# Layer 0's output projection in eight pairs of stripes with seven half-size products each, with weight sums built in DRAM during layer 0

## The chip, the cores and the metric

The kernel runs on one core of one Trainium2 chip. The metric is the device time of one execution, in microseconds (us). Before the change it is 1852.44 us, the median of three runs (1849.99 to 1852.57). The core has five engines with a queue of instructions each, and every queue runs in the order in which the program was laid out: TensorE (PE in the profile, its weight loads PEld), VectorE (DVE), ScalarE (ACT), GpSimd (POOL) and SyncE (SP). SP, ACT and POOL also issue DMAs; 16 DMA engines move the data.

## The reference, cut to what matters

Two residual layers over T = 528 tokens (16 meta tokens and 512), width D = 2048. Layer 0 is the even one; its output projection is the matrix product that the change touches.

```
def even_mixer(hn, w_in, ...):
    glu_v, glu_g, gate_a, q, c, gate_b, qi, ki, wi = split_last(hn @ w_in, EVEN_SPLITS)
    ...
    a_out = silu(layer_norm(u, ln_g, ln_b)) * silu(gate_a)        # 8 blocks of 128 features
    ...
    b_out = b_out * silu(gate_b)                                  # 8 heads of 128 features
    return concatenate([a_out, b_out], axis=-1) @ w_out           # (528 x 2048) @ (2048 x 2048)

for layer in range(DEPTH):                                        # DEPTH = 2
    hn = rms_norm(h, norm_gain[layer])
    y = even_mixer(hn, ...) if layer % 2 == 0 else odd_mixer(hn, ...)
    h = h + y
return rms_norm(h, final_norm_gain)[:, N_META:]
```

## The kernel before, in words

Activations lie transposed: 128 features on the partitions, tokens along a row. A matrix product goes by *stripes* of 128 output features. `stripe` (called with a stripe number, such as S_GA for the gates of group A or S_OE for layer 0's output projection) loads 128x2048 weights in one DMA on SP (`load_raw`, L184), takes their square sum on ACT (L192), adds it over the partitions on POOL (L144), makes a power-of-two scale from it with small DVE instructions (L148, L199, L201), and splits each half of the weights into two f16 tiles: `wh` on ACT (L208) and `wl`, the rest, on DVE (L209). The activations are split in the same way into a high and a low f16 tile (L298 on ACT, L299 on DVE). Each of the 16 k-blocks of 128 then takes three matmuls (L251, L252, L253: high by high, high by low, low by high) in each of two column halves of 264 tokens, so a stripe has 96 matmuls of 264 columns. They write PSUM tiles named `mps`, of which there are three; `s1` (four) and `po` (one) are the PSUM tiles of the attention.

Layer 0 is written as a list of steps (`EVEN`): `g` is one GLU block with its convolution of 31 DVE instructions (L584), `s` one stripe of indexer queries with its scores, `k` the top-k choice, `h` one attention head with its gate (L594, L595, tile `gb`, two buffers), `n` the layer norm of group A. Behind the list come eight gate stripes of group A (S_GA, `gate`), each with five instructions that finish `MA[i]` (L707 to L711). Then all 16 inputs of the output projection are split (`MX`, L298 and L299): eight from attention, of which six were stored to DRAM (`mbd`) by their heads and are read back on SP at L739, and eight from `MA`. Then 16 stripes of the output projection run; each adds its result onto the residual `h1` on DVE (L780), squares the new residual on ACT (L786) and sums the squares on DVE (L787). Layer 1's first two weight stripes (L271, plain f32 matmuls, 128 of them) fill the time until the row norms are there (L309, L316, L317), and L298/L299 split the inputs of layer 1.

Layer 1's own output projection already goes by pairs: `pair_stripes` takes two stripes at a time with seven products of eight k-blocks and half of the tokens each (`product`, L1154, 24 matmuls each), where two stripes in the plain way are eight such products. Four of its seven weight operands are sums of weight blocks which DMAs on POOL have built in DRAM beforehand (`os` tiles, `sum_steps`, `waves`, `send`, L347; the add happens in the DMA).

A scheduler lays the program out. Each instruction has a priority by its `band` (weights 5, evacuations 4, side work such as attention 3, convolutions and sums 2), each engine's queue is then fixed, and a queue waits at its first instruction whose input is not there. `behind(...)` places an instruction after a named earlier one.

## Time and profile before

| | |
|---|---|
| median of three runs | 1852.44 us |
| the profiled execution | 1855.38 us, its span 1853.6 us |
| PE busy | 1818.7 us (98% of the span), granted clock 0.992 on average |
| DVE busy | 1337.6 us (72%) |
| ACT busy | 1191.4 us (64%) |
| POOL busy | 183.5 us (10%) |

The profiled execution is 2.9 us above the median. Stages of layer 0 in that execution, by the windows and the chain of waits: scores, GLU and convolutions to about 350 us, heads to about 690 us with the gate stripes among the last of them, the output projection from 716.4 to 889.1 us, and the layer boundary to about 930 us. "x" before a number is a count of instructions; PEclk is the granted TensorE clock as a share of full speed. Each digit of the page's slices is the busy share of one fortieth of the span in tenths:

```profile
PE   9999999999999989999999999999999999999997
PEld 6767577788888878888777777777777765446886
DVE  7699998997646565445587777777777776757775
ACT  4845565355555876443487877778777777865562
```

### The profile page before, as it was taken

To read this page: it belongs to the slowest core of one execution; us is meant where nothing else is said; L and a number is where in the kernel's file an instruction comes from. 1 tells how busy PE (TensorE), PEld (TensorE's weight loads), DVE (VectorE), ACT (ScalarE), POOL (GpSimd) and SP (SyncE) were. 2 spreads that over 40 slices of the span, in tenths; PEclk is the share of its full clock that TensorE was granted. 3 is DMA by queue.
4 is the path that set the end of the run, shared out by engine and by line. 5 is a ranking of instruction groups with operands and counts; after the bars stand their busy time and mean duration, and the time that the engine had idled before them with its cause. 6 is when DMAs were issued, how large, how long until landed. Compare 5 with 4: busy or idle time off the path is not lost.

```text
span 1853.6 us, 36583 instructions
## 1 busy us (share of the span) xinstructions
PE 1818.7 (98%) x14870; PEld 1412.4 (76%) x14870; DVE 1337.6 (72%) x2763; ACT 1191.4 (64%) x1937; POOL 183.5 (10%) x344
## 2 busy tenths in 40 slices
PE   9999999999999989999999999999999999999997
PEld 6767577788888878888777777777777765446886
DVE  7699998997646565445587777777777776757775
ACT  4845565355555876443487877778777777865562
POOL 1100100021212012000011011010100000001000
PEclk9999999999999989999999999999999999999998
DMA  5533223234344345334465455554555344556553
GB/s 201 160 99 101 93 76 121 97 112 124 107 129 111 103 126 187 126 118 156 116 216 168 141 174 156 183 164 144 171 149 171 115 159 166 195 187 238 200 188 112
DMA packets 64856, 271.68 MB, mean 147 GB/s; under 512 B 8208, under 2 KB 15672, under 8 KB 47568
## 3 DMA queue, kind: packets, MB, share of 16 engines
q1 hardware_dynamic: 35552, 179.28, 27.6%
q0 software_dynamic: 17616, 52.19, 11.9%
q10 hardware_dynamic: 11520, 37.88, 6.1%
q8 instruction: 116, 1.90, 0.4%
q14 instruction: 52, 0.43, 0.1%
HBM read 250.76 MB, written 40.04 MB: 157 GB/s over the span
## 4 chain that ended last, share of the span: by engine, by line
PE 90%; DVE 5%; ACT 2%; DMA 1%; issue 1%; SPq 0%; POOL 0%; ACTq 0%; DVEq 0%
PE mps L251 22%; PE mps L252 22%; PE mps L253 22%; PE mps L1154 8%; PE mps L271 2%; PE po L638 1%; PE s L271 1%; PE s L613 1%; DVE mask L559 1%; DVE m L558 1%; PE s L854 1%; PE s L853 1%; DVE wl L209 1%; PE s L855 1%; PE po L976 1%; PE po L975 1%
## 5 line engine op out<-in xcount | busy, mean ns | idle before, releaser
L251 PE MATMUL mps<-x,wh 128*128 128x264 f16 (+1 forms) x3168 | 942.2, 297 | 3.2 <-ACT gt L571 1.9
L252 PE MATMUL mps<-x,wh 128*128 128x264 f16 (+1 forms) x3168 | 942.0, 297 | 0.5 <-DVE x L299 0.5
L253 PE MATMUL mps<-x,wl 128*128 128x264 f16 (+1 forms) x3168 | 941.8, 297 | 0.0
L252 PEld LDWEIGHTS <-wh 128*128 128x128 f16 x3392 | 332.7, 98 | 119.0 <-issue 6.4
L253 PEld LDWEIGHTS <-wl 128*128 128x128 f16 x3392 | 332.6, 98 | 115.4 <-issue 2.6
L251 PEld LDWEIGHTS <-wh 128*128 128x128 f16 x3392 | 332.9, 98 | 113.0 <-issue 4.0
L208 ACT ACTIVATE wh<-w,sc 128x1024 f16<-128x1024 f32 x220 | 251.1, 1144 | 198.9 <-PE mps L252 175.8
L209 DVE SCALAR_TENSOR_TENSOR wl<-w,sc,wh 128x1024 f16<-128x1024 f32 x220 | 281.1, 1280 | 104.6 <-ACT wh L208 104.4
L192 ACT ACTIVATE junk<-w 128x2048 bf16<-128x2048 f32 (+1 forms) x114 | 210.9, 1850 | 12.2 <-DMA w<-in_w_dram 8.5
L584 DVE SCALAR_TENSOR_TENSOR z<-u,vec,z 128x528 f32<-128x528 f32 x240 | 181.1, 762 | 2.3
L144 POOL PARTITION_ALL_REDUCE tot<-ss x94 | 43.3, 461 | 843.7 <-ACT junk L192 843.6
L1154 PEld LDWEIGHTS <-wh 128*128 128x128 f16 x912 | 89.2, 98 | 11.0 <-issue 0.3
L208 ACT ACTIVATE wh<-w,oq 128x1024 f16<-128x1024 f32 x53 | 60.6, 1148 | 54.6 <-PE mps L1154 46.3
L209 DVE SCALAR_TENSOR_TENSOR wl<-w,oq,wh 128x1024 f16<-128x1024 f32 x53 | 67.8, 1282 | 28.1 <-ACT wh L208 28.0
L1154 PE MATMUL mps<-on,wh 128*128 128x256 f16 x464 | 78.2, 273 | 0.1
L192 ACT ACTIVATE junk<-gw 128x1024 bf16<-128x1024 f32 x64 | 66.9, 1045 | 2.0 <-DMA gw<-in_w_dram 1.6
L850 DVE SCALAR_TENSOR_TENSOR qlm<-q,qhm 128x256 f16<-128x256 f32 x128 | 52.4, 420 | 21.3 <-ACT qhm L849 21.3
L1154 PE MATMUL mps<-on,wl 128*128 128x256 f16 x232 | 63.2, 273 | 0.0
L849 ACT ACTIVATE qhm<-q 128x256 f16<-128x256 f32 x128 | 51.0, 411 | 17.5 <-DVE q L951 16.1
L251 PE MATMUL mps<-mx,wh 128*128 128x264 f16 x224 | 61.8, 276 | 0.0
L252 PE MATMUL mps<-mx,wh 128*128 128x264 f16 x224 | 61.8, 276 | 0.0
L253 PE MATMUL mps<-mx,wl 128*128 128x264 f16 x224 | 61.8, 276 | 0.0
(438 smaller groups left out, 2898.0 us busy)
## 6 DMA issues: line engine op xcount, KB each, us to landing
w<-in_w_dram SPq DMA_DIRECT2D x132, 1024.0 KB, 4.9
gw<-in_w_dram ACTq DMA_DIRECT2D x64, 512.0 KB, 6.3
os<-in_w_dram POOLq DMA_DIRECT2D x42, 512.0 KB, 8.2
w<-os SPq DMA_DIRECT2D x28, 512.0 KB, 4.5
w<-in_w_dram SPq DMA_DIRECT2D x23, 512.0 KB, 4.6
os<-os POOLq DMA_DIRECT2D x14, 512.0 KB, 5.9
h<-in_x_dram POOLq DMA_DIRECT2D x16, 264.0 KB, 5.5
h1d<-h ACTq DMA_DIRECT2D x16, 264.0 KB, 2.3
```

Source lines behind the costliest of these rows:

```text
L144: queued["G"] = G.partition_all_reduce(out, src, channels=128, reduce_op=op or bass_isa.ReduceOp.add)
L192: S.activation(junk[:, :src.shape[-1]], src, AF.Square, accum_out=ss)
L208: queued["S"] = S.activation(hi, src, AF.Identity, scale=sc)
L209: V.scalar_tensor_tensor(lo, src, sc, hi, op0=OP.mult, op1=OP.subtract)
L251: P.matmul(o, hi[half][:, ws], xh[:, sl], start=n == 0 and k == 0, stop=False)
L252: P.matmul(o, hi[half][:, ws], xl[:, sl], start=False, stop=False)
L253: P.matmul(o, lo[half][:, ws], xh[:, sl], start=False, stop=n == 1 and k == 7)
L271: queued["P"] = P.matmul(o[:m], w32[:, k * 128:k * 128 + m], X[k][:, sl], start=k == 0, stop=k == KT - 1)
L584: eng.scalar_tensor_tensor(z, u[:, j:j + T], col(V_CW + i * CW + j), z, op0=OP.mult, op1=OP.add)
L849: S.activation(hi, src, AF.Copy, scale=scale)
L850: V.scalar_tensor_tensor(lo, src, scale, hi, op0=OP.mult, op1=OP.subtract)
L1154: P.matmul(p, wt[:, sl], xt, start=start and k == i == 0, stop=stop and k == 7 and i == 2, skip_group_check=stop and not start and resume)
```

## The change

Layer 0's output projection is made of eight pairs of stripes with seven products each. With X11, X21 the first (group A or attention) halves of the inputs and the token halves t1 and t2, the code prepares four families of f16 inputs ("forms") instead of the 16 splits: PA (attention, t1 and t1 minus t2), PB, PC (mixtures over both halves) and PD (one half), each for eight blocks. They are made block by block as the gate stripes come: `attention_form(i)` and `mixed_forms(i)` in the loop over S_GA. The attention inputs come back from `mbd` by DMAs on POOL (L783) instead of SP. The tiles of the forms are memory that earlier stages have left (`slot`, `form`).

Four weight sums per pair are built in DRAM (`esum`), by 64 DMAs on POOL (L349, 512 KB each) which `send` issues during the steps of layer 0: one or two behind each GLU, head and early score stripe, the last four among the gate stripes. The square sums of the eight gate stripes' weights and of the first two pairs' are taken ahead: 24 loads of 512 KB on the ACT queue and 24 squares of 128x1024 on ACT (`foresee`, `foreseen`), so the gate stripes get scales that are known (`known=`) and have no square and no all-reduce of their own. The scale of the mixed inputs has a factor 16 more headroom.

A pair loads and splits seven half stripes (`half_load`, `split_weights`), takes 7 x 24 matmuls of 264 columns (`product`, L910 in the new code) and adds the products onto two residuals on DVE (`add`). For pairs 2 to 7 the four loads that give the scale are squared one pair ahead (`pair_begin`, called from `pair_rest`). The residual tiles and their row-square sums are as before.

```diff
+    esum = [[dram.tile([128, 1024], F32, name=f"es{p}{i}") for i in range(4)] for p in range(8)]
...
     def glu(i):
...
+        aside(i > 3)
         ps, inv = stripe(S_GLU + 2 * i + 1, X0, back0)
+        aside(i > 3)
...
-    def gate(s, dst, keep):
-        ps, inv = stripe(s, X0, back0, keep=keep)
+    def gate(s, dst, keep=None, known=None):
+        ps, inv = stripe(s, X0, back0, keep=keep, known=known)
...
+    def foresee():
+        with band(CONV), behind("S"):
+            while seen:
+                square_sum(*seen.pop(0))
+            if left:
+                s, n = left.pop(0)
+                raw = wide()[:, :1024]
+                S.dma_start(raw, w[s, :, 1024 * n:1024 * (n + 1)])
+                seen.append((raw, gas[:, 23 - len(left):24 - len(left)]))
...
+    def aside(late):
+        send(later, min(2 if late else 1, len(later) - 4))
+        if late:
+            foresee()
...
+    later = waves(S_OE, esum, 1024)
...
+    def stage(i):
...
+        with band(SIDE), behind("B6" if i < 4 else "B7"):
+            G.dma_start(XA[i], mbd[i])
...
+    def attention_form(i):
+        x = XA[i]
+        with band(SIDE):
+            V.tensor_tensor(x[:, t2], x[:, t1], x[:, t2], op=OP.subtract)
...
+            PA[i] = split(pairs_of[-1][:, i % 2], x, mxq[1])
+
+    def mixed_forms(i):
+        x, z = XA[i], MA[i]
+        with band(SIDE):
+            PB[i] = split(form(), z, mxq[0])
+            V.scalar_tensor_tensor(z[:, t2], x[:, t2], 2.0, z[:, t2], op0=OP.mult, op1=OP.add)
+            V.scalar_tensor_tensor(x[:, t1], x[:, t1], 2.0, z[:, t2], op0=OP.mult, op1=OP.subtract)
+            V.tensor_tensor(z[:, t1], z[:, t1], z[:, t2], op=OP.subtract)
+            PC[i] = split(form(), z, mxq[0])
...
+            PD[i] = split(form(True), x[:, t1], mxq[0])
...
     for i in range(8):
         ga = et([128, T], F32, "gb", 2)
-        gate(S_GA + i, ga, stat[:, 0, i:i + 1])
+        gate(S_GA + i, ga, known=(gasc[:, i:i + 1], gainv[:, i:i + 1]))
+        send(later, 1)
+        for n in ((0, 1, 2, 3), (4,), (5,), (), (), (), (6,), (7,))[i]:
+            stage(n)
+        if i < 6:
+            attention_form(i)
...
-            if i < 6:
-                Q.dma_start(mb, mbd[i])
-            MX[8 + i] = split(r1p.tile([128, 2, T], F16, name="mx" if i < 7 else "x", bufs=7 if i < 7 else KT), mb, c[7])
-        for i in range(8):
-            MX[i] = split(r1p.tile([128, 2, T], F16, name="x", bufs=KT), MA[i], c[6])
+        if i >= 6:
+            attention_form(i)
+        mixed_forms(i)
...
-    for n in range(KT):
...
-        ps, inv = stripe(S_OE + n, MX, mback, order=(1, 0))
...
+    def pair_begin(p):
+        w11, w12, w22 = w[S_OE + 2 * p, :, 1024:], w[S_OE + 2 * p, :, :1024], w[S_OE + 2 * p + 1, :, :1024]
+        with band(WGT):
+            w11, s1 = half_load(w11), half_load(esum[p][0])
...
+                with behind("S"):
+                    for i, v in enumerate((w11, s1, w12, w22)):
+                        square_sum(v, ss[:, i:i + 1])
...
+                all_sum(one[:, 1:2], one[:, 0:1])
+                sc, inv = scales(one[:, 1:2], mback)
...
+    def pair_corner(p, raw, scale, ring):
...
+        product(a, w11, x11)
...
+        product(c, s1, y1)
...
+    def pair_rest(p, raw, scale, banks, following):
...
+            s2, w12, s3 = [split_weights(v, sc) for v in vs[:3]]
+        nxt = pair_begin(following) if following < 8 else None
+        with band(WGT):
+            s4, w22 = [split_weights(v, sc) for v in vs[3:]]
+        for bank_, wt, xs, first, dst, scl in ((b, s2, u2, True, ha[:, t2], ninv), (a, w12, x21, False, ha[:, t1], inv),
+                                               (b, s3, z3, False, hb[:, t2], inv), (c, s4, x22, False, ha[:, t2], inv),
+                                               (b, w22, z4, False, hb[:, t1], inv)):
+            product(bank_, wt, xs, start=first)
+            with band(EVAC):
+                add(dst, bank_, scl)
```

**TensorE between the attention of heads 6 and 7.** Before, these rows stand together: `po_6937` and the `s1` tiles up to 7044 belong to head 6, those from 7298 on to head 7, and `mps_7925` is the second bank of a gate stripe.

```order
L635 MATMUL s1_7021<-ident_72,L_7001 128x128
L613 MATMUL s1_7034<-Kh_6608,qh_6934 16x16
L638 MATMUL po_6937<-pt_7014,Vt_6642 128x128 [waits Activation_49]
L638 MATMUL po_6937<-pt_7014,Vt_6642 128x128 x4
L644 MATMUL s1_7040<-ident_72,L_7031 16x16 [waits Activation_49]
L648 MATMUL s1_7044<-pt_7042,Vt_6642 128x16 [waits DVE_49]
L613 MATMUL s1_7298<-Kh_6625,qh_7290 128x144 [waits PE_49]
L631 MATMUL s1_7305<-ident_72,L_7294 128x128 [waits Activation_49]
L635 MATMUL s1_7308<-ident_72,L_7294 128x128
L613 MATMUL s1_7317<-Kh_6625,qh_7290 128x272 [waits DVE_49]
L638 MATMUL po_7293<-pt_7304,Vt_6643 128x128 [waits Activation_49,Pool_49]
```

In the changed program the same places of the two heads (line numbers 8 higher) read as follows, where `mps_8041` and `mps_8175` are banks of gate stripes:

```order
L253 MATMUL mps_8041<-x_374,wl_8049 128x264
L646 MATMUL po_7119<-pt_7196,Vt_6812 128x128 [waits Activation_49]
L646 MATMUL po_7119<-pt_7196,Vt_6812 128x128 x4
L652 MATMUL s1_7222<-ident_72,L_7213 16x16 [waits Activation_49]
L251 LDWEIGHTS wh_8048
L251 MATMUL mps_8041<-x_379,wh_8048 128x264
```

```order
L253 MATMUL mps_8175<-x_339,wl_8180 128x264
L656 MATMUL s1_7226<-pt_7224,Vt_6812 128x16 [waits DVE_49]
L621 MATMUL s1_7488<-Kh_6795,qh_7480 128x144 [waits PE_49]
L251 LDWEIGHTS wh_8179
L251 MATMUL mps_8175<-x_339,wh_8179 128x264
```

Between the first piece's `s1_7222` and the second's `s1_7226` stand 27 matmuls of gate stripes, and 39 more before head 7's first transposes; before the change none stood between any of the rows shown.

**VectorE at the end of the gate stripes.** Before, the last blocks are split one behind the other (`x` tiles from `z`), with one weight split among them:

```order
L299 SCALAR_TENSOR_TENSOR x_8510<-z_4510,mxb_8443,x_8510 128x528 [waits Activation_49]
L299 SCALAR_TENSOR_TENSOR x_8513<-z_4789,mxb_8443,x_8513 128x528 [waits Activation_49]
L209 SCALAR_TENSOR_TENSOR wl_8689<-w32_8671,sc_8680,wh_8688 128x1024 [waits PE_49,Activation_49]
L299 SCALAR_TENSOR_TENSOR x_8516<-z_5425,mxb_8443,x_8516 128x528 [waits Activation_49]
L710 SCALAR_TENSOR_TENSOR z_6511<-gt_8439,z_6511 128x528 [waits Activation_49]
L595 SCALAR_TENSOR_TENSOR gb_8313<-gb_8313,gt_8432 128x528 [waits Activation_49]
L711 TENSOR_TENSOR z_6511<-z_6511,gb_8313 128x528 [waits DVE_49]
L299 SCALAR_TENSOR_TENSOR x_8519<-z_6511,mxb_8443,x_8519 128x528 [waits PE_49,Activation_49]
```

In the changed program the last two blocks' forms stand among the weight splits of the first pairs (`mb` is the attention input of heads 6 and 7; L818 to L820 are the three mixing instructions):

```order
L852 TENSOR_TENSOR z_6681<-z_6681,gb_8579 128x528 [waits DVE_49]
L299 SCALAR_TENSOR_TENSOR x_8576<-mb_7211,mxb_7599,x_8576 128x264 [waits Activation_49]
L299 SCALAR_TENSOR_TENSOR Kh_8573<-z_5554,mxb_7599,Kh_8573 128x528 [waits Activation_49]
L209 SCALAR_TENSOR_TENSOR wl_8898<-w32_8884,gaq_616,wh_8897 128x1024 [waits DMAHW6_49,PE_49,Activation_49]
L299 SCALAR_TENSOR_TENSOR Vt_8702<-z_6681,mxb_7599,Vt_8702 128x528 [waits Activation_49]
L209 SCALAR_TENSOR_TENSOR wl_8929<-w32_8884,gaq_616,wh_8928 128x1024 [waits DMAHW7_49,PE_49,Activation_49]
L818 SCALAR_TENSOR_TENSOR z_6681<-mb_7575,z_6681 128x264 [waits DVE_49]
L819 SCALAR_TENSOR_TENSOR mb_7575<-mb_7575,z_6681 128x264 [waits DVE_49]
L820 TENSOR_TENSOR z_6681<-z_6681 128x264
L209 SCALAR_TENSOR_TENSOR wl_8933<-w32_8887,gaq_616,wh_8932 128x1024 [waits DMAHW1_49,PE_49,Activation_49]
L299 SCALAR_TENSOR_TENSOR x_8576<-mb_7575,mxb_7599,x_8576 128x264 [waits Activation_49]
L299 SCALAR_TENSOR_TENSOR x_8708<-z_6681,mxb_7599,x_8708 128x528 [waits Activation_49]
```

Before, the last low half of an input followed right behind the last gate's result (L711, now L852); now seven forms and mixes and three weight splits stand between the two.

**GpSimd in the middle of the heads.** Before, biases of the attention (`L<-bdram`, then the mask added) and the all-reduces of the weights' square sums follow each other:

```order
L605 DMA L_3722<-bdram_152 128x1x272 [waits DMASW5_49,PE_49,Activation_49]
L607 DMA L_3722<-mask1_577 128x272 [waits DMASW5_49]
L605 DMA L_3743<-bdram_152 128x1x400 [waits DMASW7_49,PE_49]
L144 ISA tot_5185<-ss_5182 128x1 [waits Activation_49]
L607 DMA L_3743<-mask2_580 128x400 [waits DMASW7_49,DMASW0_49]
L502 MEMSET Vt_3858 128x128 [waits PE_49]
L144 ISA tot_5307<-ss_5304 128x1 [waits Activation_49]
```

In the changed program steps of the sums (`es`) stand among them, some of which wait for the step before them:

```order
L613 DMA L_3791<-bdram_152 128x1x272 [waits DMASW5_49,PE_49,Activation_49]
L615 DMA L_3791<-mask1_577 128x272 [waits DMASW6_49,DMASW5_49]
L613 DMA L_3812<-bdram_152 128x1x400 [waits DMASW7_49,PE_49]
L615 DMA L_3812<-mask2_609 128x400 [waits DMASW7_49,DMASW0_49]
L507 MEMSET Vt_3927 128x128 [waits PE_49]
L144 ISA tot_5302<-ss_5299 128x1 [waits Activation_49]
L349 DMA es23_194<-in_w_dram 128x1024 [waits DMASW1_49]
L349 DMA es33_198<-es31_196 16x8192 [waits DMASW2_49]
L613 DMA L_3835<-bdram_152 128x1x528 [waits DMASW3_49,PE_49,Activation_49]
L615 DMA L_3835<-mask3_612 128x528 [waits DMASW4_49,DMASW3_49]
```

Two steps of the sums now stand between an all-reduce and the bias of this head's last block of queries, and each of the two waits for an earlier DMA of this queue.

More of the change, by code (lines that the diff above doesn't have):

```diff
@@ new lines, in trunk_kernel, with form, slot, get @@
+    whole, parts = [], []
+    def form(half=False):
+        if half:
+            return parts.pop(0)
+        if not whole:
+            return xp.tile([128, 2, T], F16, name="x", bufs=KT)
+        return whole.pop(0)()
+    def slot(name, shape, bufs, dt=F32):
+        def get():
+            t = et(shape, dt, name, bufs)
+            if len(shape) > 2:
+                t = t.rearrange("p a b -> p (a b)")
+            return t[:, :T].bitcast(F16).rearrange("p (a b) -> p a b", a=2)
+        return get
@@ L700, in trunk_kernel @@
+    pairs_of = []
+    whole.extend(slot(n, [128, T], 2, F32R) for n in ("ch", "ch", "cl", "cl"))
+    KV = [slot("Kh", [128, T], 3), slot("Vt", [128, 5, 128], 3)]
+    whole.extend(KV * 2)
+    whole.extend([slot("L", [128, T], 3)] * 3 + [slot("pt", [128, 5, 128], 2)] * 2 + KV)
+    for name in ("uh", "ul"):
+        u = E.tile([128, 1024], F32R, name=name, bufs=1).bitcast(F16)
+        parts.extend(u[:, c * T:(c + 1) * T].rearrange("p (a b) -> p a b", a=2) for c in range(3))
     MA = []
@@ new lines, in trunk_kernel, with half_load, product @@
+    spare = []
+    def half_load(src):
+        if not spare:
+            t = wpool.tile([128, 2048], F32, name="w32", bufs=3)
+            spare.extend((t[:, 1024:], t[:, :1024]))
+        t = spare.pop()
+        Q.dma_start(t, src)
+        return t
+    def product(p, ws, xs, start=True, stop=True, resume=True):
+        hi, lo = ws
+        for k in range(8):
+            sl = slice(k * 128, k * 128 + 128)
+            xh, xl = xs[k]
+            for i, (wt, xt) in enumerate(((hi, xh), (hi, xl), (lo, xh))):
+                P.matmul(p, wt[:, sl], xt, start=start and k == i == 0, stop=stop and k == 7 and i == 2,
+                         skip_group_check=stop and not start and resume)
@@ new lines, in cut, with add, first_square @@
+    def cut(X, sl):
+        return [(xh[:, sl], xl[:, sl]) for xh, xl in X]
+    def add(dst, p, scale):
+        V.scalar_tensor_tensor(dst, p, scale, dst, op0=OP.mult, op1=OP.add)
+    def first_square(n):
+        nonlocal done
+        if n == 0:
+            done = S.activation(acc1, HIN[n], AF.Square)
+        else:
+            sq = U.tile([128, T], F32, name="sq1", bufs=2)
+            done = S.activation(sq, HIN[n], AF.Square)
+            V.tensor_tensor(acc1, acc1, sq, op=OP.add)
+        S.dma_start(h1d[n], HIN[n])
@@ new lines, in pair_corner @@
+    def pair_corner(p, raw, scale, ring):
+        sc, inv, ninv = scale
+        with band(WGT):
+            w11, s1 = split_weights(raw[0], sc), split_weights(raw[1], sc)
+        with band(EVAC), behind("G"):
+            while len(HIN) < min(KT, 2 * p + 4):
+                residual0()
+        ha, hb = HIN[2 * p], HIN[2 * p + 1]
+        a, b, c = [ring()[:, :HT] for _ in range(3)]
+        product(a, w11, x11)
+        with band(EVAC):
+            c1 = U.tile([128, T], F32, name="sq1", bufs=2)[:, :HT]
+            S.activation(c1, a, AF.Identity, scale=inv)
+            V.tensor_tensor(ha[:, t2], ha[:, t2], c1, op=OP.add)
+            hb2 = hb.rearrange("p (a b) -> p a b", a=2)
+            V.tensor_tensor(hb2, hb2, c1[:, None, :].to_broadcast([128, 2, HT]), op=OP.subtract)
+        product(c, s1, y1)
+        with band(EVAC):
+            add(hb[:, t2], c, ninv)
+        return a, b, c
@@ new lines, in pair_rest @@
+    def pair_rest(p, raw, scale, banks, following):
+        sc, inv, ninv = scale
+        a, b, c = banks
+        d = esum[p]
+        ha, hb = HIN[2 * p], HIN[2 * p + 1]
+        with band(WGT):
+            vs = [half_load(v) if p < 2 or i in (0, 2, 3) else v
+                  for i, v in enumerate((d[1], raw[2], d[2], d[3], raw[3]))]
+            s2, w12, s3 = [split_weights(v, sc) for v in vs[:3]]
+        nxt = pair_begin(following) if following < 8 else None
+        with band(WGT):
+            s4, w22 = [split_weights(v, sc) for v in vs[3:]]
[3 more added lines that the diff above has]
+            product(bank_, wt, xs, start=first)
+            with band(EVAC):
+                add(dst, bank_, scl)
+                if wt is s4:
+                    first_square(2 * p)
+                elif wt is w22:
+                    first_square(2 * p + 1)
+        return nxt
@@ new lines, in trunk_kernel @@
+    mback = mxq[2]
+    done = None
+    H1 = HIN
+    x11, y1 = cut(PA, t1), cut(PA, t2)
+    x21, x22 = cut(PB, t1), cut(PB, t2)
+    z4, u2 = cut(PC, t1), cut(PC, t2)
+    z3 = PD
+    begun = [pair_begin(0), pair_begin(1)]
+    banks = [pair_corner(p, *begun[p], (bank, ps1)[p]) for p in range(2)]
+    for p in range(8):
+        if p > 1:
+            banks.append(pair_corner(p, *begun[p], bank))
+        nxt = pair_rest(p, *begun[p], banks[p], p + 2 if p == 0 else p + 1 if p > 1 else 8)
+        if nxt:
+            begun.append(nxt)
```

177 lines of the change are left out of this document (100 added, 77 removed).

## The prediction, as put on record

> **What bounds the kernel now.** I read the page's totals first, then the chain that ended last, then the windows of layer 0's end.
>
> ```profile
> span 1853.6 us, 36583 instructions
> PE 1818.7 (98%) x14870; PEld 1412.4 (76%) x14870; DVE 1337.6 (72%) x2763; ACT 1191.4 (64%) x1937; POOL 183.5 (10%) x344
> PE 90%; DVE 5%; ACT 2%; DMA 1%; issue 1%; SPq 0%; POOL 0%; ACTq 0%; DVEq 0%
> ```
>
> TensorE is busy for 98% of the span and makes 90% of the chain, so a matmul that goes away is worth its time wherever TensorE is the limit. Whether it is, has to be read stage by stage: columns are the stretch, its length, busy us and (instructions) of each engine, the granted clock, the DMA share and GB/s.
>
> ```profile
> 90.00:275.00 185.00, 181.93 (x1235) 127.12 (x1232) 178.18 (x316) 106.98 (x177) 21.01 (x33) 0.98 0.29 92
> 350.00:690.00 340.00, 331.25 (x2773) 285.91 (x2774) 235.52 (x494) 208.96 (x400) 59.56 (x95) 0.98 0.40 114
> 630.90:716.40 85.50, 80.83 (x658) 69.32 (x657) 48.03 (x108) 63.83 (x123) 18.94 (x34) 0.94 0.47 145
> 716.40:889.10 172.70, 172.70 (x1538) 150.20 (x1536) 79.95 (x137) 76.31 (x83) 7.94 (x19) 1.00 0.39 133
> 889.10:930.00 40.90, 40.33 (x184) 29.81 (x182) 25.89 (x44) 20.60 (x29) 4.51 (x8) 1.00 0.41 125
> ```
>
> The output projection is the row from 716.4 to 889.1: TensorE busy in all of it, at full clock, VectorE and ScalarE under half. The row ahead of it, head 7 and the gate stripes, has 4.7 us without matmuls and a clock of 0.94. From 90 to 275 us VectorE is nearly as full as TensorE (178.18 of 185).
>
> **The products: −21.6 us.** 16 stripes of 96 matmuls are 1536, in 172.70 us with two others: 0.1123 us each. Eight pairs of seven products of 24 matmuls, also 264 columns wide, are 1344. 192 fewer, at 0.1123 us, are 21.6 us. This holds if nothing else limits the new stage. The nearest stage that runs so is layer 1's output projection, with pairs and seven products of 256 columns:
>
> ```profile
> 1690.00:1830.00 140.00, 139.86 (x1279) 125.02 (x1278) 101.14 (x129) 80.03 (x91) 2.12 (x4) 1.00 0.53 183
> L208 ACT ACTIVATE wh<-w,sc 128x1024 f16<-128x1024 f32 x220 | 251.1, 1144 | 198.9 <-PE mps L252 175.8
> L209 DVE SCALAR_TENSOR_TENSOR wl<-w,sc,wh 128x1024 f16<-128x1024 f32 x220 | 281.1, 1280 | 104.6 <-ACT wh L208 104.4
> L192 ACT ACTIVATE junk<-gw 128x1024 bf16<-128x1024 f32 x64 | 66.9, 1045 | 2.0 <-DMA gw<-in_w_dram 1.6
> L780 DVE SCALAR_TENSOR_TENSOR h<-mps,inv,h 128x264 f32<-128x264 f32 x31 | 15.3, 492 | 29.2 <-PE mps L253 29.2
> L787 DVE TENSOR_TENSOR acc<-acc,sq 128x528 f32<-128x528 f32 x14 | 9.8, 702 | 1.4 <-ACT sq L786 1.4
> L786 ACT ACTIVATE sq<-h 128x528 f32<-128x528 f32 x14 | 8.8, 629 | 9.1 <-DVE h L780 9.1
> ```
>
> It shows no stall (139.86 of 140.00). Layer 0's pair has more beside it. TensorE takes 168 × 0.1123 = 18.9 us for a pair. VectorE: seven splits at 1.280 are 9.0 us, six additions at 0.492 are 3.0, two sums of squares at 0.702 are 1.4, the two instructions that spread the first product about 1.2 (one like L780, one like L787), and the small ones of the scale below 1: 15 to 15.6 us. ScalarE: seven splits at 1.144 are 8.0, four squares at 1.045 (5.0 with their readouts, at most 0.2 each), two row squares at 0.629 are 1.3, one evacuation 0.5: some 14.8 us. Both fit under 18.9, with a fifth to spare. I take no stall; what happens if that cover is gone is a rival below.
>
> **The hole between heads 6 and 7: −7 us.** Before, TensorE loses time in the gate stripes:
>
> ```profile
> 658.00:662.00 4.00, 2.61 (x21) 1.96 (x19) 1.13 (x6) 2.00 (x5) 1.46 (x2) 1.00 0.06 18
> 662.00:666.00 4.00, 2.73 (x13) 2.40 (x13) 1.06 (x5) 1.07 (x5) 1.23 (x3) 0.59 0.47 121
> 666.00:670.00 4.00, 1.99 (x7) 1.56 (x8) 2.88 (x8) 2.98 (x8) 1.38 (x2) 0.50 0.67 154
> 670.00:674.00 4.00, 4.00 (x23) 3.07 (x22) 3.54 (x9) 3.93 (x10) 0.84 (x2) 0.63 0.53 121
> ACT gb L594 <- DVE mb L649: 3.3, 1, 3.3
> PE s L631 <- ACT L L622: 9.0, 5, 2.8
> ```
>
> Busy time by granted clock is 2.61 + 2.73 × 0.59 + 1.99 × 0.50 + 4.00 × 0.63 = 7.7 us of full-speed work in 16 us, so 8.3 us are lost. The last two rows (time, times, longest) say why: a gate tile `gb` waits until head 6 has given one back, the gate stripe's second bank waits for it, and meanwhile TensorE's queue holds only the short dependent matmuls of the attention, each waiting for ScalarE's softmax. In the changed order 27 gate matmuls stand between two of these steps and 39 behind them, 66 × 0.1123 = 7.4 us of work. So the holes have something in them. I take 7; the bounds are 0, if those matmuls find their banks or weights not ready, and 8.3.
>
> Beside these rows stands a rule of the Trainium skill, page "TensorE: Matmul & The Clock Gate", Part 1 (the HAM clock gate): after about 3.4 us of an idle window the clock goes to half, and about 3.4 us of work bring it back. The rows with 0.59 and 0.50 agree with it, and by it a filled hole returns all of the slow matmuls, so that this term would be −8.3 and the sum 1.3 us lower; a new wait of that length would cost 1.7 us more than itself (half of 3.4, an estimate).
>
> **The forms: +5 us.** Rows for their prices, two of them from layer 1's forms of 256 columns, and the reload of an attention block (KB, us to landing):
>
> ```profile
> L298 ACT ACTIVATE x<-z,mxb 128x528 f16<-128x528 f32 x7 | 4.6, 719 | 0.0
> L299 DVE SCALAR_TENSOR_TENSOR x<-z,mxb,x 128x528 f16<-128x528 f32 x7 | 4.9, 761 | 1.2 <-ACT x L298 1.2
> L1061 DVE TENSOR_TENSOR on<-on 128x256 f32<-128x256 f32 x3 | 1.3, 425 | 0.1
> L1063 DVE TENSOR_TENSOR on<-on,on 128x256 f32<-128x256 f32 x3 | 1.3, 418 | 0.0
> Kh<-mbd SPq DMA_DIRECT2D x3, 264.0 KB, 2.6
> ```
>
> For each block VectorE does three wide low halves (3 × 0.761 = 2.3 us), one narrow one and four narrow mixes (five instructions; 0.42 from layer 1's rows to 0.49 from L780, so 2.1 to 2.5). Eight blocks are 35 to 38 us; the 16 old low halves at 0.761 were 12.2. So 23 to 26 us are added. ScalarE gets three wide and one narrow, 2.6 × 8 = 21 us, for 16 × 0.719 = 11.5, and loses the eight full squares of the gate stripes. On the whole stage from 630.9 to 716.4, VectorE's 48.03 us become 71 to 74 in the 78.5 us that are left without the hole: it fits, at over 90%. But the mixes cannot be spread: the changed order puts 111 VectorE instructions from the end of head 6's attention to the last form, worth 60 to 66 us at this trace's durations for each kind, against some 61 us of matmuls up to the product that needs that form. Two waits more stand on this path. VectorE's subtraction on a reloaded attention block is queued behind a DMA that GpSimd issues only after head 7's last bias, and all of VectorE's queue waits with it (the same reload took 2.6 us to land from SP's queue; I allow 2 to 3.5); and the last low half comes after three weight splits (3 × 1.280). Bounds: 0, when the order's excess is absorbed by the two corners of products that run first on attention forms alone (96 matmuls, 10.8 us), and 12, when the excess of 6, the wait of 3.5 and one more round of 2.5 add up. I take 5, nearest the order's own sum.
>
> **The sums in DRAM and the early squares: +3 us.** Prices per transfer:
>
> ```profile
> q1 hardware_dynamic: 35552, 179.28, 27.6%
> q0 software_dynamic: 17616, 52.19, 11.9%
> q10 hardware_dynamic: 11520, 37.88, 6.1%
> L347 POOL DMA_DIRECT2D os<-in_w_dram x42: 521/838/1118, 872.1 to 1418.0; - x42
> DMA to landing us min/median/max: 4.2/7.8/11.0
> 1260.00:1280.00 20.00, 20.00 (x219) 16.25 (x218) 17.22 (x45) 15.78 (x28) 2.44 (x5) 1.00 0.71 219
> POOL L L607 <- DMA L<-bdram: 67.9, 26, 4.6
> ```
>
> GpSimd's queue (q0) takes 11.9% of 1853.6 us for 52.19 MB, 4.2 us of all 16 engines per MB; 64 steps of 0.52 MB are 141 us. ScalarE's queue (q10) takes 3.0 us per MB; 24 loads are 38 us. Nearly all falls between 230 and 690 us. There DMA is at 0.40, so it goes to some 0.8. The row at 1260 us has 0.71 with TensorE busy throughout, and it has the same kind of sums in it; nothing shows 0.8 held for long. GpSimd issues 64 more, 0.84 us each at the median: 54 us on a queue that was busy for 60 of 340 us. Behind them wait the all-reduces of weight scales and the biases, which already wait 67.9 us on their DMAs in 26 cases. ScalarE's 24 squares are 30 us more of 340, where it is busy for 209. Weights are loaded ahead, so most of this is covered; where cover is thin (90 to 275 us, VectorE full) only single steps are sent. Bounds: −2, since 8 all-reduces leave the weights' path, and +12, an added 0.5 us for each of the 24 stripes sent past. I take 3, nearest to layer 1's rows without a stall.
>
> **Layer boundary: −0.6 us.** The boundary row has 0.57 us without a matmul, a wait for the first input of layer 1. Part of the 128 plain matmuls now precede the last products, and the norm comes earlier in their run, so this wait goes. That is all there is to gain: TensorE is full otherwise.
>
> **Sum.** The profiled execution has 1855.4: −21.6 −7 +5 +3 −0.6 gives 1834.2. It lies 2.9 above the median of the runs, 1852.4; so the forecast for the median is **1831 us**. A measurement of this kernel can tell about 0.2%, 3.7 us, from no change.
>
> **Rivals.**
> *The hole stays.* `gb` still has two buffers, held by heads 6 and 7, and three `mps` banks are all there are. If the gate matmuls' banks wait as before, the 7 are not gained: 1838. Against it stands the new order with its 66 fillers. Chance 0.15.
> *The forms bound the stage harder.* VectorE at 12 us over, and a clock that falls in the wait (4 us at 0.63, as in the row at 670 us, lose 1.5): 1831 + 7 + 1.5 = 1840, and to 1846 with more such waits. For it: the order's sums have VectorE at 100% for 60 us. Chance 0.15.
> *The pair stage is bound by VectorE and ScalarE.* If each of six pairs waits for its scale (square, all-reduce, three small instructions, then a split, nothing overlapped: about 1.5 to 2.5 us each), 9 to 15 us come back: 1840 to 1846. Against it: squares are taken one pair ahead. Chance 0.09.
> *The DRAM building costs more than the products save.* Place: GpSimd's queue among the heads. Each of the 24 stripes with sums behind them has 10.8 us (96 × 0.1123) for its 1 MB load (2.8 to 3 us of the engines), two sums (4.4), an early load (1.6) and the biases: about 9 of 10.8. If steps wait in order for the step before (7.8 us to landing at the median) ahead of a bias or an all-reduce, a stripe is late by what is over. From 1.0 us on each of the 24 on, in place of the 3 counted, the gain is gone: 1831 + 21 = 1852, and at 1.2 us it is 1857, slower. For it: the waiting steps stand right ahead of biases. Against it: layer 1 hides 56 steps. Chance 0.08.
> The Trainium skill, page "DMA: Bandwidth & Descriptors", section "SWDGE vs HWDGE vs iDMA", says that a VectorE instruction in its two-port mode locks GpSimd out of the memory in which it writes descriptors. By that, issues would be longest where VectorE is fullest; the 521 to 1118 ns of the row above leave room for that, and 64 times the spread of 0.6 us would be 38 us of GpSimd (an estimate), which points to the rival just named.
> *All goes better*: hole and boundary gained, forms and sums free: 1820. Chance 0.08.
>
> **How the numbers follow.** The forecast, 1825 to 1837, has 0.45. With the two rivals at 1838 to 1846, most of the pair stage's and half of the better case it makes 0.8 to 0.85 from **1819 to 1848**. Faster by over 0.2% are all cases but the DRAM rival and the tails of two others that add up: 0.87; within 0.2%: 0.05; slower: 0.08.
>
> **What would show it.** The projection in about 151 us with TensorE full is the first step; a window without the half clock in the gate stripes the second; TensorE waiting for low halves of inputs from VectorE at the first products the third, 5 us in all; and first product and heads reached no later than before, apart from 3 us, the fourth. It is wrong if TensorE waits for weights or biases among the heads, or for weight splits in the pairs.

## The result, and the profile after

The changed kernel takes 1871.38 us in the median (1865.51 to 1880.11, four runs) against 1851.93 us before (now four runs): a ratio of 1.0111, 95% interval 1.007 to 1.0151. It is slower by 1.1%, and lies far above the range. Its profiled execution has a span of 1870.0 us, 16.4 above the one before. From the page of the changed kernel, the totals, the queues and the chain:

```profile
span 1870.0 us, 36551 instructions
PE 1808.0 (97%) x14678; PEld 1395.5 (75%) x14678; DVE 1392.1 (74%) x2836; ACT 1232.4 (66%) x2033; POOL 219.5 (12%) x398
...
q0 software_dynamic: 25520, 87.37, 19.7%
...
PE 61%; issue 4%; DVE 3%; ACT 3%; DMA 2%; POOL 1%; SPq 0%; DVEq 0%; ACTq 0%; POOLq 0%
```

The 192 matmuls are gone (14870 to 14678), yet TensorE stands idle for 62 us in place of 35, and its part of the chain is 61% in place of 90%. Where, the windows say. First before (from the heads to the layer boundary), then after, cut at the first product of the projection (716.4 and 742.0 us); columns as in the prediction:

```profile
290.00:400.00 110.00, 101.22 (x860) 85.60 (x859) 103.05 (x245) 49.32 (x76) 13.42 (x21) 0.98 0.33 101
400.00:640.00 240.00, 240.00 (x2050) 208.90 (x2049) 159.68 (x324) 150.26 (x293) 41.85 (x68) 1.00 0.39 114
640.00:716.40 76.40, 71.72 (x579) 61.18 (x577) 44.80 (x102) 54.73 (x103) 18.73 (x34) 0.93 0.52 162
889.10:950.00 60.90, 60.33 (x345) 44.04 (x343) 42.03 (x84) 40.60 (x66) 7.38 (x13) 1.00 0.48 160
```

```profile
290.00:400.00 110.00, 89.70 (x727) 74.63 (x728) 91.57 (x231) 51.49 (x84) 19.70 (x32) 0.93 0.70 190
400.00:640.00 240.00, 229.58 (x1915) 196.62 (x1914) 161.12 (x332) 141.28 (x285) 59.09 (x94) 0.98 0.73 194
640.00:742.00 102.00, 101.73 (x872) 88.30 (x870) 68.95 (x137) 72.07 (x145) 14.70 (x24) 1.00 0.42 130
742.00:890.00 148.00, 145.49 (x1282) 125.74 (x1281) 117.26 (x181) 98.43 (x131) 7.75 (x16) 1.00 0.69 230
890.00:950.00 60.00, 55.05 (x302) 40.89 (x301) 36.81 (x67) 33.33 (x46) 9.16 (x16) 0.97 0.56 172
```

The end of the gate stripes is full now at full clock: the hole is gone. The pair stage has 2.5 us idle. But in the heads TensorE does 727 and 1915 matmuls where it did 860 and 2050, so that the first product comes 25.6 us late; and the layer boundary, which had 0.6 us idle, has 5.0, at a clock of 0.97. VectorE's longest waits on DMAs and on GpSimd in the first 745 us (us in total, times, longest) are these:

```profile
DVE L L623 <- DMA L<-mask: 21.7, 5, 6.1
DVE u L148 <- POOL tot L144: 18.5, 15, 5.3
```

Before, in the first 720 us, they were these:

```profile
DVE L L615 <- DMA L<-mask: 3.4, 3, 2.4
DVE u L148 <- POOL tot L144: 8.8, 14, 1.4
```

### The profile page after: what moved, and what is told of

It reads as the page before. It is cut to its first block, busy times and chain, and to the rows that moved or that the text cites. A ratio compares the mean times of both kernels' runs of the same rounds, so it can differ in the third digit from the quotient of the medians.

```text
span 1870.0 us, 36551 instructions
## 1 busy us (share of the span) xinstructions
PE 1808.0 (97%) x14678; PEld 1395.5 (75%) x14678; DVE 1392.1 (74%) x2836; ACT 1232.4 (66%) x2033; POOL 219.5 (12%) x398
## 4 chain that ended last, share of the span: by engine, by line
PE 61%; issue 4%; DVE 3%; ACT 3%; DMA 2%; POOL 1%; SPq 0%; DVEq 0%; ACTq 0%; POOLq 0%
PE mps L252 13%; PE mps L253 13%; PE mps L251 13%; PE mps L910 13%; DMA w<-in_w_dram 1%; PE po L1208 1%; PE po L646 1%; PE po L1207 1%; PE s L1085 1%; PE s L1086 1%; PE s L1087 1%; DVE wl L209 1%; ACT junk L192 1%; PE s L910 1%; PE s L621 1%
## 5 line engine op out<-in xcount | busy, mean ns | idle before, releaser
L251 PE MATMUL mps<-x,wh 128*128 128x264 f16 (+1 forms) x2880 | 865.5, 301 | 13.0 <-ACT gt L577 7.2
L252 PE MATMUL mps<-x,wh 128*128 128x264 f16 (+1 forms) x2880 | 865.5, 301 | 1.7 <-DVE x L299 1.7
L253 PE MATMUL mps<-x,wl 128*128 128x264 f16 (+1 forms) x2880 | 865.6, 301 | 0.0
L252 PEld LDWEIGHTS <-wh 128*128 128x128 f16 x2880 | 283.4, 98 | 125.0 <-issue 20.0
L253 PEld LDWEIGHTS <-wl 128*128 128x128 f16 x2880 | 283.4, 98 | 110.4 <-issue 5.4
L251 PEld LDWEIGHTS <-wh 128*128 128x128 f16 x2880 | 283.5, 98 | 106.0 <-issue 4.5
L208 ACT ACTIVATE wh<-w,sc 128x1024 f16<-128x1024 f32 x214 | 243.6, 1144 | 137.6 <-PE mps L252 85.8
L209 DVE SCALAR_TENSOR_TENSOR wl<-w,sc,wh 128x1024 f16<-128x1024 f32 x214 | 272.7, 1279 | 50.7 <-ACT wh L208 48.6
L192 ACT ACTIVATE junk<-w 128x2048 bf16<-128x2048 f32 (+2 forms) x114 | 190.8, 1674 | 24.9 <-DMA w<-in_w_dram 23.5
L910 PEld LDWEIGHTS <-wh 128*128 128x128 f16 x1808 | 176.8, 98 | 26.5 <-ACT wh L208 1.4
L144 POOL PARTITION_ALL_REDUCE tot<-ss x78 | 36.6, 469 | 701.5 <-ACT junk L192 701.5
L910 PEld LDWEIGHTS <-wl 128*128 128x128 f16 x904 | 88.5, 98 | 13.1 <-issue 1.2
L910 PE MATMUL mps<-on,wh 128*128 128x256 f16 x464 | 78.2, 273 | 0.1
L910 PE MATMUL mps<-on,wl 128*128 128x256 f16 x232 | 63.2, 273 | 0.0
L209 DVE SCALAR_TENSOR_TENSOR wl<-w,gsc,wh 128x1024 f16<-128x1024 f32 x32 | 41.0, 1282 | 27.2 <-ACT wh L208 27.2
L627 ACT ACTIVATE L<-L,st 128x144 f32<-128x144 f32 (+4 forms) x40 | 20.7, 517 | 53.4 <-DVE st L623 53.4
```

The costliest lines, as they stand in the source:

```text
L144: queued["G"] = G.partition_all_reduce(out, src, channels=128, reduce_op=op or bass_isa.ReduceOp.add)
L192: S.activation(junk[:, :src.shape[-1]], src, AF.Square, accum_out=ss)
L208: queued["S"] = S.activation(hi, src, AF.Identity, scale=sc)
L209: V.scalar_tensor_tensor(lo, src, sc, hi, op0=OP.mult, op1=OP.subtract)
L251: P.matmul(o, hi[half][:, ws], xh[:, sl], start=n == 0 and k == 0, stop=False)
L252: P.matmul(o, hi[half][:, ws], xl[:, sl], start=False, stop=False)
```

## The experiments

**First: is it the sums, and which property of them?** Theory Q: sum steps stand ahead of the attention's biases in GpSimd's DMA queue. Theory B: all 16 DMA engines are too busy. Theory O: the other laid-out order and the early squares. Four kernels.

e1_nosums:

```diff
-    esum = [[dram.tile([128, 1024], F32, name=f"es{p}{i}") for i in range(4)] for p in range(8)]
+    esum = [[w[S_OE + 2 * p + i % 2, :, 1024 * (i // 2):1024 * (i // 2) + 1024] for i in range(4)] for p in range(8)]
-    later = waves(S_OE, esum, 1024)
+    later = []
```

> The changed kernel without the 64 DMAs that build sums in DRAM during layer 0; the pairs load blocks of the weights in place of the sums, so the output projection's values are left wrong and its loads, splits and products stay. Theory Q (the sums stand ahead of the attention's biases and the scores' copies in GpSimd's DMA queue, and these land late) and theory B (all 16 DMA engines are too busy for them) both expect the first product at 712 to 720 us in place of 742, and 1842 to 1850 us in all. Theory O (the other laid-out order, and the early squares on ScalarE, lose the time) expects the first product at 735 or later and 1865 us or more.

1843.24 us (ratio to before 0.9947, 0.9932 to 0.9962), the first product at 713.5 us. The sums cost 28 us, all of it ahead of the first product; theory O falls as the cause by itself.

e2_copies_pool and e3_copies_act: 64 plain copies at the same places, on GpSimd's and on ScalarE's queue.

```diff
+    later = [(dram.tile([128, 1024], F32, name=f"cp{i}"), w[S_OE + i % 16, :, 1024 * (i % 2):1024 * (i % 2) + 1024], 0)
+             for i in range(64)]
...
-                G.dma_start(dst, src, accum_op=OP.add if add else OP.bypass)
+                S.dma_start(dst, src)                     # e3 alone
```

> As e1, but at the same 64 places plain copies of 512 KB from DRAM to DRAM on GpSimd's queue, each to its own place, so that none adds and none waits for another (the pairs read weight blocks, the output projection's values are left wrong). Theory Q expects most of the loss: 1860 to 1872 us. Theory B the same, less what the reading of the target for the addition takes: 1858 to 1870. If only the waits of one step for the step before cost time, 1842 to 1850.

1844.66 us (0.9953, 0.9934 to 0.9971). The same number of transfers of the same size, from the same queue at the same places, cost 1.4 us in the medians, less than the spread of e2's runs (1841.80 to 1848.94). Both theories expected 1858 us or more. So neither a DMA share of 0.65 to 0.68 in the heads nor a DMA's mere place in the queue is the loss by itself.

> As e2, the same 64 copies at the same places, issued on ScalarE's queue in place of GpSimd's. Theory Q expects the loss to go: 1842 to 1852 us, with the biases landing in 2.2 to 3.6 us as before. Theory B expects no difference from e2: 1858 to 1870.

1923.79 us, a failed experiment: in its first 100 us the DMA share is 0.99 and TensorE is busy for 51 us. Nothing held the copies back on ScalarE's queue: they were issued between 0.8 and 112 us, beside the inputs' loads. It says nothing on the question.

e4_before_plus_sums adds `send(later, ...)` with `later = waves(S_OE, esum)` to the kernel before at the places of the change (the steps add other halves of the weights).

> The kernel before with nothing but the 64 sum DMAs added, at the places where the change has them (nothing reads them). Theories Q and B expect the whole loss of the heads on top of before: the first product of the output projection at 735 to 750 us in place of 716, and 1872 to 1886 us. Theory O expects 1850 to 1856.

1861.75 us (1.0054, 1.0034 to 1.0074): the sums alone cost 9 us there, a third of the 28 and less than theories Q and B expected. Its trace does not show where: the profiled execution, 1855.51 us, is the fastest of four (the others 1861.61 to 1866.23), and has the first product at 716.5 us, as before. So something else in the change makes the sums dear.

**Second: additions or waits?** e5_steps_plain changes one flag. Every engine's queue, with its waits, reads the same as in the changed kernel, row by row.

```diff
-                G.dma_start(dst, src, accum_op=OP.add if add else OP.bypass)
+                G.dma_start(dst, src, accum_op=OP.add if add and todo is not later else OP.bypass)
```

> The changed kernel with the same 64 DMAs, places, waits and instruction order on every engine, but each step a plain copy in place of an addition (the sums, and with them the output projection's values, are left wrong). Theory A (the additions themselves load the DMA engines and GpSimd's queue more than copies do) expects 1843 to 1850 us, as with the independent copies. Theory D (steps that wait for the step before hold up GpSimd's queue, or the laid-out order is bad) expects what the change has, 1865 to 1875.

1845.89 us (0.9962, 0.9950 to 0.9974), the first product at 715.2. With the instruction order held fixed, 32 additions cost 25.5 us more than 32 copies do. What differs is seen in the issues (ns min/median/max) of the steps; first the changed kernel, then e5:

```profile
L349 POOL DMA_DIRECT2D es<-in_w_dram x48: 533/873/1297, 49.2 to 617.3; - x48
```

```profile
L349 POOL DMA_DIRECT2D es<-in_w_dram x48: 515/547/574, 49.0 to 588.1; - x48
```

and in the queues' shares of 16 engines over 745 us and the biases' time to landing, again the change and then e5:

```profile
q0 software_dynamic: 16944, 51.11, 30.1%
...
L<-bdram POOLq DMA_DIRECT2D x8, 264.0 KB, 6.4
...
L<-bdram POOLq DMA_DIRECT2D x8, 72.0 KB, 5.4
```

```profile
q0 software_dynamic: 17104, 51.65, 24.0%
...
L<-bdram POOLq DMA_DIRECT2D x8, 264.0 KB, 4.6
...
L<-bdram POOLq DMA_DIRECT2D x8, 72.0 KB, 3.8
```

The additions hold the engines for 6.1% of 745 us longer, 45 us or 1.4 us each, at nearly the same megabytes (51.11 and 51.65). Of the 48 issues in the first two rows 32 add: their record lasts 890 ns in the median, and 544 ns as copies. But the next step behind one of them starts after 549 to 591 ns in the change and after 538 to 560 ns in e5, so GpSimd's queue is hardly held up by the issue itself. The 32 adding steps land after 8.0 us in the median, the same 32 as copies after 6.3. Since the order is the same, the two traces can be laid over each other: VectorE's delay grows in a few jumps. The first is at 302 us (4.7 us), four more like it come at 331, 359, 392 and 575 (2.8, 1.8, 2.3 and 3.0), each at `L623`, an attention step that waits for its bias with the mask added. Here GpSimd's and VectorE's timelines of the change around the first (start, duration, idle time before and what ended it):

```profile
289.99 0.86 POOL L349 DMA_DIRECT2D es<-in_w_dram  x1
290.54 0.83 POOL L349 DMA_DIRECT2D es<-es  x1
295.15 0.90 POOL L615 DMA_DIRECT2D L<-mask  x1 [3.78 <-DVE mask L567]
```

```profile
302.56 0.31 DVE L623 CUSTOM_DVE_ANT_0 L<-s,L 128x144 f32<-128x144 f32 x1 [5.20 <-DMA L<-mask]
```

The mask's addition, issued at 295.15, lands at 302.43; in e5 the same DMA takes 2.5 us, and VectorE waits 0.46. The two steps ahead of it landed at 296.13 and 297.33. In the 5.1 us after that the engines work for a weight load on SP and hardly for GpSimd's queue. The load's issue, and the queues' shares from 297.4 to 302.4 us:

```profile
295.96 0.33 SPq L187 DMA_DIRECT2D w<-in_w_dram  x1
```

```profile
q1 hardware_dynamic: 136, 0.98, 51.9%
q0 software_dynamic: 23, 0.01, 1.8%
```

In e5 the mask's addition landed 1.6 us after the last step and 1.7 us after this load was issued. So it reads as if the longer steps had pushed the mask's addition in among the load. At 331, 359 and 392 us it lands 0.7 to 1.3 us after the last step ahead of it, at 575 us 10.3 us after. While VectorE waits at 302 us, its queue holds top-k work, which could have run, behind the instruction that waits.

The second kind of jump, 1.1, 1.5, 1.9 and 4.6 us at 428, 458, 490 and 521 us, has one more link. GpSimd's own queue waits, for the bias, with the mask's addition, and an all-reduce of weights' square sums stands behind it. In the change, and then in e5:

```profile
519.49 0.89 POOL L615 DMA_DIRECT2D L<-mask  x1 [10.69 <-DMA L<-bdram]
520.13 0.89 POOL L613 DMA_DIRECT2D L<-bdram  x1
520.78 0.60 POOL L144 PARTITION_ALL_REDUCE tot<-ss  x1
```

```profile
495.83 0.91 POOL L615 DMA_DIRECT2D L<-mask  x1 [4.43 <-DMA L<-bdram]
496.48 0.88 POOL L613 DMA_DIRECT2D L<-bdram  x1
498.65 0.38 POOL L144 PARTITION_ALL_REDUCE tot<-ss  x1 [1.29 <-ACT junk L192]
```

In e5 the all-reduce comes as soon as ScalarE's square is there; in the change it starts 4.5 us after the square's end (516.29 us), and a weight's scale, both halves' splits and TensorE wait with it. That bias was issued at 508.24 behind two steps, which landed at 514.18 and 517.57; it landed at 519.21, after 11.0 us. The nine jumps make 23.6 of the 26.8 us by which the first product is later than in e5. In six of them (14.0 us) the bias or mask lands 0.3 to 2.4 us after the last step ahead of it in its queue. In the other three, at 302, 490 and 575 us (9.6 us), the last step had landed 5 to 10 us before it, and weight loads of other queues were under way. So theory A is shown (additions cost, copies do not), and theory Q has the place right for the larger part: a bias or mask waits for the steps ahead of it, and adding steps are slow ones. That the rest comes from loads that share the engines is read from the traces and was not tried by itself.

**Third: why 28 us here and 9 on the kernel before?** e6_noforesee has the sums without the early loads and squares, e9_neither has neither, x2_loads_nosquares has the loads without the squares (which, with e1, makes a table).

```diff
-    left = [(S_GA + i, n) for i in range(8) for n in range(2)] + [(S_OE + i, n) for i in range(4) for n in range(2)]
+    left = []                                             # e6 and e9; x2 keeps the loads and drops square_sum
-            V.tensor_reduce(gasum[:, sl], src, axis=AX, op=OP.add)
-            all_sum(gasum[:, sl], gasum[:, sl])
+            V.memset(gasum[:, sl], 128.0 if sl.start == 0 else 256.0)
```

> The changed kernel with its 64 sums, without the 24 early loads, squares and all-reduces (scales from constants near the true sums take their place; this leaves that part of the computation out). Theory I (the early loads and squares and the sums together are too much, each alone is not) expects 1843 to 1855 us. Theory A or D, sums alone: 1862 or more.

> The changed kernel with neither the 64 sums nor the 24 early loads and squares (weight blocks in place of sums, constants in place of the scales' sums; the output projection's values are left wrong). It is the fourth corner beside the change (both), e1 (early loads alone) and e6 (sums alone). If the two only cost together, it is as e1, 1841 to 1845 us, and the sums cost 10 to 14 us without the early loads and 28 with them. If the early loads cost by themselves, it is below 1838.

> The change with its 64 sums and its 24 early loads, without the 24 early squares and the all-reduces behind them (the scales come from constants, as in e6; that part of the computation is left out). If the early loads' traffic is what makes the sums dear (e6, without either, has the first product at 721 us and 1854.6 us; the change at 742 and 1871): 738 to 744 and 1866 to 1874 us. If it is the squares in ScalarE's queue: 718 to 724 and 1850 to 1857 us.

| first product at, us; median of the runs, us | no sums | sums |
|---|---|---|
| no early loads | 713.9; 1849.27 (e9) | 721.1; 1854.59 (e6) |
| early loads alone | | 734.6; 1867.11 (x2) |
| early loads and squares | 713.5; 1843.24 (e1) | 742.0; 1871.38 (the change) |

By the first product, the early loads and squares cost nothing by themselves (713.9 and 713.5), the sums 7.2 us by themselves, and 28.5 us with the loads and squares: 21 us more. The loads make 13.5 of the 20.9 us by which the first product moves between e6 and the change, the squares with their all-reduces the other 7.4. By the medians these are 12.5 and 4.3 us, and the runs of x2 (1861.46 to 1871.03) and of the change (1865.51 to 1880.11) overlap, so the second part is not clear of noise. e6 is where it was expected if only both together are too much. e9 is 6 us slower than e1, outside both of its expected ranges; all of that lies behind the first product, where e9's row norms come 8.6 us later (181.6 us after the first product against 173.0). It is not the worth of scales known ahead, for e9 has its scales from constants. These kernels are laid out in different orders, so the parts are less sure than e5's.

**Fourth: the layer boundary.** In the changed kernel's ScalarE timeline a square for a later weight stripe stands ahead of the first inputs of layer 1, and waits for its load; and the inputs come in twos with VectorE's next two behind them, since the change left two `sq1` buffers of three:

```profile
916.29 1.91 ACT L192 ACTIVATE junk<-w 128x2048 bf16<-128x2048 f32 x1 [4.38 <-DMA w<-in_w_dram]
...
918.20 1.35 ACT L298 ACTIVATE x<-sq,gains 128x528 f16<-128x528 f32 x2
...
925.06 1.36 ACT L298 ACTIVATE x<-sq,gains 128x528 f16<-128x528 f32 x2 [2.43 <-DVE sq L1033]
```

The row norms were there at 911.9, and the first high half starts at 918.2. e8_bound is e1 with two edits against this:

```diff
-            with behind("S"):
+            with behind(held.pop(0) if held else "S"):
                 square_sum(w32, ss)
...
-            t = U.tile([128, T], F32, name="sq1", bufs=2)
+            t = U.tile([128, 1024], F32, name="w4", bufs=4)[:, :T]
             V.tensor_tensor(t, H1[n], rstd1, op=OP.mult)
+            queued["X"] = queued["H"] if n == 11 else queued.get("X")
...
+    held.extend(("S", "S", "X"))
```

> The kernel of e1 (no sums, weight blocks in their place, output left wrong) with two edits at the layer boundary: the normalised tiles take four buffers (w4) in place of two (sq1), and the square of the third weight stripe of layer 1 stands behind the twelfth of the sixteen high halves in ScalarE's queue. If the boundary's loss comes from these two, TensorE's waits for x there (some 4.7 us) go: 1836 to 1839 us, after e1's 1843. If another thing delays the inputs of layer 1, 1842 to 1845.

1836.05 us (0.9909, 0.9893 to 0.9925), 7.2 less than e1. Which of the two edits brings it was not tried. The boundary of e1, then the pair stage and the boundary of e8, cut at the same distances from their first products (713.5 and 713.3 us) as the change's rows above:

```profile
861.50:921.50 60.00, 53.96 (x272) 38.56 (x271) 38.06 (x69) 31.46 (x42) 9.25 (x16) 0.94 0.58 175
```

```profile
713.30:861.30 148.00, 145.41 (x1276) 125.46 (x1275) 115.92 (x179) 98.42 (x131) 7.83 (x16) 0.99 0.68 226
861.30:921.30 60.00, 60.00 (x358) 46.68 (x358) 42.21 (x80) 40.60 (x59) 10.67 (x16) 1.00 0.63 199
```

The boundary is full at full clock; the pair stage keeps its 2.6 us without matmuls.

**Fifth: can the whole change be made to pay?** All have e8's boundary edits. v1_spread sends two steps where the change sends one and one where it sends two; v2_spread_ownsq also lets the gate stripes square their own weights; v3_bias_act moves the biases' loads to ScalarE's queue; v4_late sends none among heads 0 to 2 and 16 among the gate stripes.

```diff
-        send(later, min(2 if late else 1, len(later) - 4))
+        send(later, min(1 if late else 2, len(later) - 4))                      # v1, v2
+        send(later, min(2 if not late else 1 if len(Z) > 4 or busy[0] > 2 else 0, len(later) - 16))  # v4
-            queued[f"B{h}"] = G.dma_start(e[:nq, :W], bias_rows(h, q0, nq, 0, W))
+            queued[f"B{h}"] = S.dma_start(e[:nq, :W], bias_rows(h, q0, nq, 0, W))  # v3
```

> The whole change with all sums and right values, the two edits at the layer boundary of e8, and the sums sent earlier: two behind each score stripe and each of the first GLU stripes in place of one, one behind each later stripe in place of two. If the sums cost where they stand ahead of biases among the heads, 1846 to 1858 us. If they cost the same wherever they are sent, 1862 to 1866, the change less the 7 us of the boundary.

1854.15 us (1.0003, 0.9991 to 1.0015): less the boundary's 7, spreading returns 10 of the 28 us.

> As v1, and the gate stripes square their own weights again (16 of the 24 early loads and squares are gone, eight full squares and all-reduces are back). If sums and early loads only cost together: 1836 to 1848 us. If the early loads are without effect once the sums are spread: as v1.

1858.76 us (1.0031, 1.0021 to 1.0042): not faster than v1, against the expectation. Why is open.

> The whole change with right values and the boundary edits, the sums where the change has them, and the attention's bias loads issued on ScalarE's queue in place of GpSimd's (the mask's additions stay on GpSimd's). If the loss comes from biases that stand behind sum steps in GpSimd's DMA queue, 1842 to 1854 us. If the masks' additions suffer alike, or ScalarE's queue is held up by the biases' waits for a free buffer, 1860 or more.

1872.95 us (1.0104, 1.0088 to 1.0120): nothing gained, and 9 us more than the change less the boundary's 7. The masks' additions are still in GpSimd's queue behind the steps (VectorE waits 15.7 us for them), and one bias lands 9.5 us after its issue on ScalarE's queue. This run gives theory Q no support, and with the masks left behind the steps it does not refute it.

> The whole change with right values and the boundary edits, and the sums sent elsewhere: two behind each score and early GLU stripe (32), none among heads 0 to 2, where VectorE is full, one behind each later stripe (16) and two behind each gate stripe (16). If the wait for late biases costs most where VectorE is full (290 to 400 us), TensorE is busy there for 98 to 101 us of 110, as without sums, and the time is 1842 to 1850 us. If the additions cost wherever biases follow them, as v1, 1851 to 1858.

1857.32 us (1.0020, 1.0006 to 1.0033). TensorE is busy for 97.7 us of the 110 from 290 to 400, near the 98 expected. The loss has moved to where the steps went: by 290 us v4's TensorE has done 57 matmuls fewer than e8's, and from 400 to 640 us 65 fewer. So clearing the heads where VectorE is full is not enough. None of the whole versions beats the kernel before.

## Why the prediction was wrong, point by point

- **The sums, the step that failed.** The prediction added +3 us with bounds from −2 to +12; they cost 28 (change against e1). It priced them as throughput: engine time per megabyte against a share of 0.8, and issues against an idle GpSimd queue. Both were about right (the share was 0.70 to 0.73), and neither gives the cost. The price is latency: the attention's short DMAs, issued behind adding steps, land late, after those steps (14.0 us of the overlay's 23.6) or in among a weight load (9.6 us), and VectorE's and GpSimd's queues stop at them. The rival on GpSimd's queue among the heads named this place and a time of 1852 to 1857 us, but had a chance of 0.08, because layer 1 hides 56 steps. Layer 1's stage with sums has no chain like bias, mask and softmax through the same DMA queue: in the profile before, GpSimd issues no DMA but the 56 steps from 870 to 1440 us. That difference could be read there, in the 67.9 us that the masks' additions waited for biases.
- **Additions and copies.** The prediction had one price for all steps, 4.2 us per MB. e5 shows that the adding half takes 1.4 us more each and lands 1.7 us later.
- **The early squares.** Without sums they are covered, as predicted: the first product is at 713.5 us with them and at 713.9 without (e1, e9). That they multiply the sums' cost, from 7 to 28 us, was no step of the prediction.
- **The layer boundary.** Predicted −0.6, because the norm comes earlier; the runs show +7.2 (e1 to e8). The norm did come early (row norms 9.9 us behind the last product, 17.4 before), and ScalarE's queue was the next to be late, with a square that waits for its load. The change cut the `sq1` buffers from three to two; the prediction did not count it.
- **The hole.** Predicted −7. It is closed (101.73 of 102.00 us at full clock). The half clock of 662 to 674 us went with it, as the rule of the Trainium skill, page "TensorE: Matmul & The Clock Gate", Part 1, has it. But e8 reaches the first product only 3.1 us earlier than before, so some 5 us of the 8.3 are lost again ahead of it: e8's TensorE is 21 matmuls behind the kernel before at 290 us, 44 at 400 and 53 at 640, some 6 us at 0.1123 us each (an estimate). Why was not tried.
- **The products and the forms.** Predicted −21.6 and +5. From first product to the end of the span e8 takes 1121.4 us and the kernel before 1137.2: 15.8 less, where the prediction had 17.2 less with its boundary term. The pair stage has 2.6 us without matmuls in e8 and 2.5 in the change, all near its start; of these the products wait 1.1 us for the low half of a form, where the prediction expected 5. VectorE and ScalarE did not become the bound (115.92 and 98.42 us of 148 in e8).
- **GpSimd's issues.** The page "DMA: Bandwidth & Descriptors" of the Trainium skill, section "SWDGE vs HWDGE vs iDMA", has VectorE's two-port mode lock GpSimd out of its descriptors. No run here shows it: as copies, the steps take 515 to 574 ns to issue beside the same VectorE instructions. The spread of 521 to 1118 ns that the prediction read as room for it is additions (812 to 1118 ns, 28 of the 42) and copies (521 to 847) side by side.
- **The sum.** Without sums and without the boundary's loss the prediction's terms give 1828 us, and e8 takes 1836. Of the 8 us, 3.9 are the hole's and 1.4 those of the products, forms and boundary together; most of the rest is how the profiled executions stand to their medians (2.9 us above it before, 0.9 in e8). The other 35 us, from e8 to the change, are the two terms that failed: 28 for the sums and 7 for the boundary.

## What to carry to other kernels

Here a short DMA behind bulk ones was priced by when it landed, not by the share of the engines: before bulk transfers are put on a queue, look for a chain of short DMAs on it that an in-order engine waits for, and for the loads of other queues that meet them. Adding DMAs and plain copies are priced apart, and one run with the flag flipped, which leaves the order as it was, shows the difference. When the first wait at a boundary goes, read in which queue the next instruction stands, and count the buffers that the diff takes away.

## What the runs showed of the hardware that was not expected

A DMA that adds 512 KB onto DRAM has an issue record of 890 ns in the median where a copy of the same size has 544, takes 1.4 us more of the 16 engines and lands 1.7 us later. The change's four runs lie 14.6 us apart, e1's four without the steps 2.3, e5's ten with copies 9.8. Sixty-four copies of 512 KB beside the heads cost 1.4 us in the medians (e2 against e1, within the spread of the runs) at a DMA share of 0.65 to 0.68.
